# A recurrence's first stage moved beside the former pair's inverse: a re-ordered RWKV-7 hybrid step on one core

## The chip, the core and the metric

The kernel runs on one core of a Trainium2 chip. The metric is the device time of one launch in microseconds (us). Three runs of the kernel before gave 1659.1, 1659.86 and 1661.35 us; their median, 1659.86 us, is the time before. One further execution was profiled and took 1659.02 us.

## The reference, cut to what matters

One layer of a decoder trunk for 1024 prompt positions and 8 x 8 sample positions, 1088 columns in all, D = 1024, all in float32:

```python
h = rms_norm(x, norm_mix) * (1 + sc) + sh
P = h @ w_in                                   # RWKV columns, pooling columns, gates
xl = pr + (pr_prev - pr) * mu_shift
r, k, v, xw, xa, xg = split(xl)
decay = exp(-exp(-softplus(-(w0 + tanh(xw) @ w2)) - 0.5))
a = sigmoid(a0 + xa @ a2)
kk = heads(k * k_k);  kk = kk * rsqrt(sum(kk * kk) + 1e-12)
k = k * (1 + (a - 1) * k_a)
# per position t and head, state S (64 x 64):
S = S * w_t + (S @ -kk_t) (kk_t * a_t)^T + v_t k_t^T;   y_t = S r_t
# group norm of y, bonus, gate; merge with the pooling branch; w_out; then the MLP
```

What the change touches is the part from `k`, `xw` and `xa` to the products that the state update needs: the norm of `kk`, the two tanh of the low-rank maps (`w2` and `a2`), the running sums of the decay inside chunks of 64 positions, and the scaled copies of `k`, `kk * a`, `r` and `kk`.

## The kernel before, in words

Everything lies with features on the 128 partitions and positions along the free dimension. A large product is made from three matmuls on split operands (a rounded part `whi` and the rest `wlo`, lines 193 and 194), 362 or 364 columns at a time. These are called dense work here.

**Phase 1** streams w_in (34 blocks of 128 output columns, two weight halves each) and then the pooling half of w_br. **Phase 2** streams the other half of w_br, w_out and the MLP. The recurrence runs inside phase 1. It takes the 8 heads as four pairs, f = 0 to 3 (64 + 64 partitions), and the prompt as 16 chunks of 64 positions; the sample positions are a 17th chunk.

**The order of the work.** The order of TensorE's instructions is the program's own (`tc.manual_schedule(engines={PE})`), and a small planner writes it. `Pace.run` has one backlog of dense work and four generators: `chains`, `heads`, `pools` and `or_rows`. It keeps a clock `t`, to which each matmul adds an estimated cost. A generator that yields a number becomes due that many nanoseconds later on this clock; one that yields a condition becomes due when it holds. Whoever is due is resumed, the first in the list first; if nobody is due, the backlog emits three more matmuls. `warm(t)` is a condition that waits for `t` nanoseconds and for enough matmul work in the last 3400. The order on the other engines and on the DMA queues is made by the compiler's scheduler from the instructions as they were emitted.

**One pair.** `heads` (line 1143) goes through the pairs one after the other. For pair f:

- `lead` is `front(f)` and then `scores(f)`. Beside it runs `sample(f - 1)`, the sample positions of the pair before.
- `front` (line 648) loads `k`, `xw` with `xa`, and `r` from scratch memory; squares `k` (line 660), makes the norm by 18 narrow matmuls in `rinv` (line 345), spreads it by 9 transposes (line 177) and multiplies (line 672); makes the two low-rank maps in three column pieces with two tanh each (lines 677 and 680); waits for `("c", f - 1, 0)`, the end of the first half of the former pair's chain; and then emits, without a pause, the burst: for each half of the columns a sum (697), a scan (698), two or three Exp on ScalarE (700 to 703), and seven more VectorE instructions (706 to 711). After the first half `ra` (line 724) makes the first operands of `scores`. Its last step loads `v` and multiplies `q` (721).
- `scores` runs unit 0, the bonus, unit 2 (the sample chunk) and unit 1. Unit 0 starts its first matmul 9000 ns after `ra`.
- Then `main`, which is `inverse` (15 short VectorE steps), `level` (four rounds of 32 x 32 matmuls) and `affine` (`first` and `second` for each half), runs beside a fill: `post(f - 1)` for the former pair's group norm and gate, or `ada_fill` for f = 0. `both` is the helper that runs two generators side by side.
- `chain(f)` (line 964) steps the state through the 16 chunks, one step each 2300 ns of the planner's clock (line 994).

At the end come `sample(3)` and `post(3)`.

**Buffers.** The small products write PSUM tiles with the tag `w`, of which there are two; dense work has four (`mm`), and the chain has two (`wc`). `wt` is a ring of five 128 x 1088 tiles that `front`, `post` and the bonus share. `bk` and `e` have one buffer each; `ra` of the prompt has two.

## Time and profile before

| What | Value |
|---|---|
| median of 3 runs | 1659.86 us |
| the profiled execution | 1659.02 us |
| its span, first to last instruction | 1657.2 us |
| mean granted TensorE clock | 0.990 |
| TensorE busy (matmul) | 1599.2 us, 96% |
| VectorE busy | 1034.0 us, 62% |
| ScalarE busy | 712.7 us, 43% |

Each row of a view tells one thing. "PE" is TensorE's matmuls, "DVE" VectorE, "ACT" ScalarE, "POOL" GpSimd, "SP" the queue that issues most DMAs. In a timeline a row is: start in us, duration in us, engine, line, operation, output<-inputs, shapes, count, and in brackets the engine's idle time before it with what ended it. In a table by stretches the columns are: the stretch, its length, the busy time of each engine with its instruction count, the granted share of the TensorE clock, the share of the DMA engines and GB/s. In a table of waits: who waited <- for whom: us in total, times, longest.

### The profile page before, as it was taken

How to read it: one execution, taken by the hardware profiler on the slowest of the kernel's cores; microseconds unless marked ns; L12 is line 12 of the kernel's file. 1: busy time of each engine (PE TensorE's matmuls, PEld its weight loads, DVE VectorE, ACT ScalarE, POOL GpSimd, SP SyncE). 2: the span in 40 equal slices, each digit the busy share in tenths (PEclk: the TensorE clock that was granted, in tenths of full speed). 3: DMA queues.
4: the chain of work that ended last, by engine and by line, in shares of the span. 5: the costliest groups of instructions: out<-in, count | busy, mean ns of one | idle time of the engine just before them, and what ended most of it. 6: DMA issues, size and time to landing. Idle time of an engine off the chain costs nothing.

```text
span 1657.2 us, 35379 instructions
## 1 busy us (share of the span) xinstructions
PE 1599.2 (96%) x14331; PEld 1490.2 (90%) x14331; DVE 1034.0 (62%) x1800; ACT 712.7 (43%) x1378; POOL 354.5 (21%) x459
## 2 busy tenths in 40 slices
PE   6999999999999999999999999999999999999997
PEld 3989888887888889979989999999999999999997
DVE  5686547744675456335545596777555667776866
ACT  5543333344334334412224376455444656552323
POOL 3310111110000000000631333323233343521221
PEclk9999999999999999999999999999999999999999
DMA  9333413331322142375975455666766866574313
GB/s 337 112 110 133 139 53 117 114 105 64 115 107 101 70 149 88 117 294 177 330 280 195 144 186 172 234 227 232 238 218 212 311 202 217 174 257 167 98 39 109
DMA packets 123332, 279.42 MB, mean 169 GB/s; under 512 B 16769, under 2 KB 31105, under 8 KB 123169
## 3 DMA queue, kind: packets, MB, share of 16 engines
q1 hardware_dynamic: 107808, 228.52, 40.4%
q0 software_dynamic: 9312, 32.41, 6.0%
q10 hardware_dynamic: 6048, 16.23, 2.8%
q8 instruction: 113, 1.85, 0.5%
q14 instruction: 51, 0.41, 0.1%
HBM read 198.15 MB, written 78.95 MB: 167 GB/s over the span
## 4 chain that ended last, share of the span: by engine, by line
PE 59%; POOL 2%; DVE 2%; issue 2%; DMA 2%; ACT 1%; DVEq 0%; SPq 0%; POOLq 0%; ACTq 0%
PE pr L170 32%; PE mm L170 20%; PE w L170 5%; PE wc L170 2%; POOL t L1367 1%; POOL wlo L194 1%; DMA wraw<-in_w_ff 1%; DMA hid<-in_w_ada_mlp 0%; DMA hid<-d_th 0%; PE w L177 0%; DVE hx L1898 0%; DMA wr<-in_w_ff 0%; ACT whi L193 0%; POOL hx L1336 0%; DMA wraw<-in_w_br 0%
## 5 line engine op out<-in xcount | busy, mean ns | idle before, releaser
L170 PE MATMUL mm<-hx,whi 128*128 128x362 f32 (+1 forms) x1920 | 507.9, 346 | 6.2 <-ACT px L564 2.9
L170 PEld LDWEIGHTS mm<-hx,whi 128*128 128x128 f32 x1920 | 334.1, 190 | 42.6 <-issue 18.0
L170 PE MATMUL pr<-mr,whi 128*128 128x272 f32 x1792 | 337.5, 287 | 1.0 <-ACT whi L193 0.7
L170 PE MATMUL mm<-hx,wlo 128*128 128x362 f32 (+1 forms) x960 | 316.2, 329 | 0.0
L170 PEld LDWEIGHTS pr<-mr,whi 128*128 128x128 f32 x1792 | 281.7, 189 | 3.1 <-issue 2.2
L170 PE MATMUL pr<-mr,wlo 128*128 128x272 f32 x896 | 258.5, 289 | 2.8 <-DVE wlo L194 2.8
L193 ACT ACTIVATE whi<-wraw 128x512 fp32r<-128x512 f32 x186 | 116.7, 629 | 251.3 <-PE mm L170 73.4
L170 PEld LDWEIGHTS mm<-hx,wlo 128*128 128x128 f32 x960 | 182.9, 191 | 0.0
L194 DVE TENSOR_TENSOR wlo<-wraw,whi 128x512 fp32r<-128x512 f32 x145 | 108.8, 751 | 106.0 <-ACT whi L193 105.0
L170 PEld LDWEIGHTS pr<-mr,wlo 128*128 128x128 f32 x896 | 169.3, 189 | 3.0 <-DVE wlo L194 3.0
L170 PE MATMUL pr<-hx,whi 128*128 128x272 f32 x896 | 168.7, 287 | 1.4 <-DVE rs L1924 0.8
L170 PE MATMUL mm<-mr,whi 128*128 128x272 f32 (+4 forms) x736 | 152.7, 302 | 0.7 <-DVE t L1363 0.7
L170 PEld LDWEIGHTS pr<-hx,whi 128*128 128x128 f32 x896 | 140.3, 188 | 2.6 <-ACT whi L193 1.0
L193 ACT ACTIVATE whi<-wr 128x512 fp32r<-128x512 f32 x138 | 86.2, 628 | 128.7 <-PE pr L170 94.0
L170 PE MATMUL pr<-hx,wlo 128*128 128x272 f32 x448 | 128.9, 288 | 0.0
L170 PEld LDWEIGHTS mm<-mr,whi 128*128 128x128 f32 x736 | 119.2, 188 | 4.9 <-issue 3.4
L170 PE MATMUL mm<-mr,wlo 128*128 128x272 f32 (+4 forms) x368 | 110.1, 299 | 0.0
L194 POOL TENSOR_TENSOR wlo<-wraw,whi 128x512 fp32r<-128x512 f32 x41 | 55.6, 1356 | 250.7 <-ACT whi L193 250.4
L194 DVE TENSOR_TENSOR wlo<-wr,whi 128x512 fp32r<-128x512 f32 x103 | 77.4, 755 | 16.7 <-ACT whi L193 16.4
L170 PE MATMUL pr<-t,whi 128*128 128x272 f32 x448 | 84.6, 287 | 0.0
L170 PEld LDWEIGHTS pr<-hx,wlo 128*128 128x128 f32 x448 | 84.3, 188 | 0.0
L170 PEld LDWEIGHTS pr<-t,whi 128*128 128x128 f32 x448 | 70.2, 188 | 0.8 <-issue 0.8
(398 smaller groups left out, 2681.2 us busy)
## 6 DMA issues: line engine op xcount, KB each, us to landing
wr<-in_w_ff SPq DMA_DIRECT2D x137, 256.0 KB, 3.5
hid<-d_ch POOLq DMA_DIRECT2D x72, 272.0 KB, 4.2
wraw<-in_w_ff SPq DMA_DIRECT2D x71, 256.0 KB, 3.2
wraw<-in_w_in SPq DMA_DIRECT2D x68, 256.0 KB, 2.9
d_ch<-hx SPq DMA_DIRECT2D x52, 272.0 KB, 3.7
hid<-in_w_ada_mlp SPq DMA_DIRECT2D x24, 512.0 KB, 6.5
d_th<-px SPq DMA_DIRECT2D x22, 544.0 KB, 2.9
wt<-d_x SPq DMA_DIRECT2D x20, 544.0 KB, 4.1
```

The costliest lines, as they stand in the source:

```text
L170: return self.nc.tensor.matmul(out, lhsT, rhs, **kw)
L193: nc.scalar.activation(hi, raw, AF.Copy)
L194: (nc.gpsimd if pool else nc.vector).tensor_tensor(lo, raw, hi.bitcast(F32), op=ALU.subtract)
L1367: (nc.vector if m == 7 else nc.gpsimd).tensor_tensor(t, t, S["u"], op=ALU.add)
```

## The change

`front` is cut in two. What loads, norms and makes the tanh stays `front`; the burst becomes a generator of its own, `burst`, which for f > 0 yields between its steps. `heads` runs `front(0)` ahead of the loop and `front(f + 1)` behind `post(f - 1)` in the fill beside `main`; the lead is then `burst(f)` and `scores(f)`. The pause after each tanh piece is 2600, 1900 and 1900 ns for 1300 three times. For f > 0 the wait for the former pair's chain and the first `ra` stand at the end of the burst, and unit 0 starts 3000 ns after it for 9000. In `affine`, one of the three copies out of PSUM goes from VectorE to ScalarE.

```diff
             nc.scalar.activation(tha[:, c0:c0 + n], ps[:, :n], AF.Tanh, bias=self.hp[:, 4 + f:5 + f], scale=0.5)
-            yield 1300
+            yield 1900 if c0 else 2600
         yield X(f)
         r = self.wt()
         nc.sync.dma_start(r, self.d_x[f])
+        self.cur = dict(k=k, kk=kk, t1=t1, tha=tha, r=r)
+
+    def burst(self, f):
+
+        nc, io = self.nc, self.io
+        X = lambda b: lambda: ("X", b) in self.done
+        k, kk, t1, tha, r = (self.cur[x] for x in ("k", "kk", "t1", "tha", "r"))
+        step = lambda t: t if f else 0
         e = self.row(self.p1, "e", 1, w=1112)
...
-        if f:
-            yield lambda: ("c", f - 1, 0) in self.done
         for c0, n in FH:
...
             nc.vector.tensor_tensor_scan(t, self.kscan[:, s], t, 0.0, ALU.mult, ALU.add)
+            yield step(1800)
...
             for h, hs in enumerate(HB):
+                yield step(1700)
                 nc.vector.tensor_tensor(bk[hs, cs, h, :], cut(x[hs]), cut(t[hs]), op=ALU.mult)
...
             if c0 == 0:
                 self.cur = dict(bk=bk, end=end, kk=kk, r=r, ev=ev, es=es, z=self.z, qs={})
-                self.ra(self.cur, 0)
+                if f == 0:
+                    self.ra(self.cur, 0)
+            yield step(1400)
...
         self.cur.update(q=q, v=v)
+        if f:
+            yield lambda: ("c", f - 1, 0) in self.done
+            self.ra(self.cur, 0)
...
-        yield 9000 if u == 0 else 3000 if u == 1 else 2000
+        yield (3000 if f else 9000) if u == 0 else 3000 if u == 1 else 2000
...
-            nc.vector.tensor_copy(uv[HB[1], :, 0, :], cut(pu[HB[1], :]))
+            nc.scalar.activation(uv[HB[1], :, 0, :], cut(pu[HB[1], :]), AF.Copy)
...
+        yield from self.front(0)
         for f in range(4):
             def lead():
-                yield from self.front(f)
+                yield from self.burst(f)
                 yield from self.scores(f, self.cur)
...
-            fill = self.post(f - 1) if f else self.ada_fill()
             self.ds[f] = d
+
+            def fill():
+                yield from self.post(f - 1) if f else self.ada_fill()
+                if f < 3:
+                    yield from self.front(f + 1)
...
-            yield from self.both(main(), fill)
+            yield from self.both(main(), fill())
```

## The prediction, made before the changed kernel ran

> **What bounds the kernel now.** First the page, its part on busy time.

> ```profile
> PE 1599.2 (96%) x14331; PEld 1490.2 (90%) x14331; DVE 1034.0 (62%) x1800; ACT 712.7 (43%) x1378; POOL 354.5 (21%) x459
> ```

> TensorE (PE) works almost all the time, and the change takes no matmul away and adds none. So nothing can be won but time in which PE waits, or in which its clock is not granted in full; a shorter recurrence does not pay by itself. That second point must be checked at the end of phase 1, in the timelines of DVE and PE there.

> ```profile
> 775.73 0.76 DVE L1133 TENSOR_TENSOR hx<-wt,hx 128x576 fp32r<-128x576 f32 x1 [0.75 <-ACT hx L1132]
> ...
> 784.38 0.49 PE L170 MATMUL w<-hx,whi 128*128 128x362 f32 x2
> ```

> The recurrence's last result is written at 776.5 us; the first product that reads such rows (its third chunk goes to a `w` tile) is there at 784.38, some 8 us later. If the recurrence ends earlier nothing is won, and if it ends more than about 8 us later PE is left without work.

> Next the view by stretches: the three leads, from the end of `affine` of pair f - 1 to unit 0 of pair f, and a stretch that is nearly all dense.

> ```profile
> 219.00:264.00 45.00, 41.08 (x340) 32.84 (x338) 33.08 (x60) 17.74 (x38) 7.27 (x10) 0.96 0.20 64
> 385.00:429.20 44.20, 38.57 (x308) 29.90 (x306) 27.74 (x51) 16.25 (x33) 2.44 (x3) 0.92 0.30 97
> 545.50:592.50 47.00, 44.79 (x380) 36.24 (x379) 28.70 (x56) 16.53 (x35) 0.73 (x2) 0.93 0.20 65
> 740.00:780.00 40.00, 40.00 (x245) 39.02 (x244) 20.50 (x35) 10.27 (x18) 3.84 (x3) 1.00 0.53 182
> ```

> In the leads PE is idle for 3.9, 5.6 and 2.2 us, 11.7 in all, and the clock (the column behind POOL) sinks to 0.96, 0.92 and 0.93. The dense stretch has neither. What PE waited for over the whole span, and three of these waits in PE's timeline:

> ```profile
> PE w L170 <- ACT wt L677: 5.7, 8, 2.0
> PE wc L170 <- DVE S L994: 4.3, 4, 2.8
> PE mm L170 <- ACT px L564: 2.9, 3, 1.8
> ...
> PE w L170 <- DVE wt L1115: 1.9, 2, 1.0
> ...
> PE mm L170 <- ACT px L582: 1.6, 1, 1.6
> ...
> PE w L170 <- ACT at L944: 0.6, 1, 0.6
> ```

> ```profile
> 244.98 0.33 PE L170 MATMUL w<-x,z 64*64 64x64 f32 x4 [2.05 <-ACT wt L677]
> ...
> 425.15 0.48 PE L170 MATMUL wc<-S,ra 64*64 64x64 f32 x4 [2.80 <-DVE S L994]
> ...
> 581.24 0.34 PE L170 MATMUL w<-ab,uv 128*64 128x64 f32 x4 [0.58 <-ACT wt L677]
> ```

> The first three rows are the leads' causes. The two `w` tiles are held until the tanh of line 677 has read them: six of the eight waits, from 244.98 to 581.24, are those of the sample's products, the other two stand in the first front. The chain's step (line 994) stands behind the burst on DVE. And dense chunks are copied out late by ACT (564). Where the clock is lost, by stretches on PE:

> ```profile
> 220.00:240.00 20.00, 20.00 (x139) 0.91 0.19 62
> 234.00:237.40 3.40, 3.40 (x19) 0.50 0.14 50
> 401.20:404.60 3.40, 3.40 (x19) 0.50 0.64 204
> 425.10:428.50 3.40, 3.35 (x17) 0.50 0.75 199
> 561.65:568.48 6.83, 6.83 (x31) 0.50 0.04 14
> ```

> Four stretches at half clock in the leads: 17.0 us, so at most 8.5 us lost.

> **The change, part by part.** The sum is made against the profiled execution: 1659.02 us, of which 1657.2 are span and 1.8 lie around it. It stands 0.8 us under the median of the runs, 1659.86.

> *The front moves.* PE's timeline shows where it stands and where it can go.

> ```profile
> 359.53 0.27 PE L177 MATMUL w<-kct,sw 128*128 128x128 f32 x1
> ...
> 382.02 0.28 PE L170 MATMUL w<-ab,at 64*64 64x128 f32 x2
> ...
> 393.62 2.06 PE L170 MATMUL w<-kct,wt 128*128 128x2 f32 x18
> ...
> 412.79 0.76 PE L170 MATMUL w<-wt,sw 64*128 64x288 f32 x4
> ```

> `post` of pair 0 has its last transpose at 359.5 and its last writes some 3 us later; `affine` of pair 1 ends at 382, the next front's norm is at 393.6, its last tanh piece at 412.8, unit 0 at 429.2. After the change the front starts behind `post`, so its norm comes near 374 (11.6 us after its start, as now from 382 to 393.6). Its last piece is 19 us later, and 2.5 us more for the longer pauses: near 395, where the lead starts. The burst's pauses are 2 x (1.8 + 1.7 + 1.7 + 1.4) = 13.2 us, with each of the eight resumptions half a microsecond late some 17; then 3 us to unit 0: near 415, 14 us earlier than 429. Over three pairs the recurrence gets some 35 to 40 us shorter, which is worth nothing at the end of phase 1: the same dense work stands alone behind it. The loads hardly move, since the compiler has them ahead already, in the queue's timeline:

> ```profile
> 364.11 0.42 SPq L658 DMA_DIRECT2D wt<-d_x x1
> ```

> This load of `k` is issued 29 us before the norm at 393.62. I cost the DMAs at nothing: the five `wt` tiles are taken in the same order as before, and what SP holds behind a late load is the next weights, of which two are ahead; if that cover fails, it costs the dense work 1 or 2 us a pair.

> *Waits that go.* (a) The tanh's waits: beside the burst, which uses no `w`, the sample meets none, and the first front has the longer pauses: -5.7 us, between 0 and -5.7. (b) The chain's step waits because the whole burst was emitted ahead of it on DVE; in steps, it leaves room: -4.3, 0 to -4.3. (c) Dense chunks copied late are half a matter of what ACT happens to do: -1.4, 0 to -2.9. (d) The clock: the stretches at 234 and 561 follow the front's 18 narrow matmuls, those at 401 and 425 the stalls of 1.8 and 2.8 us. The narrow matmuls stay, the stalls should go; I take half, -4, between 0 and -8.5.

> [...]

> (e) The copy of line 945, by its own entry and that of the ScalarE copy behind it:

> ```profile
> L945 DVE COPY uv<-w x8: 694/695/695, 202.6 to 701.0; 64x512 f32<-64x512 f32 x8
> L946 ACT ACTIVATE uv<-w x8: 585/590/592, 203.4 to 701.8; 64x512 f32<-64x512 f32 x8
> ```

> 0.69 us on DVE become 0.59 on ACT, eight times. Behind it on ACT stand copies of dense chunks, for which PE waited 1.6 us once (line 582). ACT now does three copies in a row, but needs no longer wait for DVE between two of them: -0.5, from -1.6 to +2.

> *Waits that come.* (f) The front's ten `w` tiles a pair now meet `affine`, each stage of which takes both: the same kind of collision with another partner. Nothing before shows it; the nearest rows are the tanh's 5.7 us in all, and the waits of `post` and `affine` beside each other (1115, 944), 0.6 to 1.0 us each. I take two a pair at 1 us, +6, the row nearest to it; between 0 and +16 (five a pair). (g) The lead becomes short for DVE; I take +2, from 0 to +17, as weighed below. The wait for the former chain, moved behind the burst, has only `ra` and unit 0 queued behind it in its generator; where it comes late, it delays the recurrence, which has those 35 us to spare, and PE does dense work meanwhile: nothing.

> Sum: -5.7 - 4.3 - 1.4 - 4 - 0.5 + 6 + 2 = -7.9 us: 1651.1 for an execution like the profiled one, 1651.9 beside the median. **I predict 1651.5 us.**

> **The rivals.** *DVE becomes the bound of the lead* (slower). In the lead at 385 DVE is busy for 27.74 us; some 2 us of it, the norm's multiplies, move out with the front. The lead shrinks to 20 us. If the burst began only with it, DVE would be 27.7 - 2 - 20 = 5.7 us behind at unit 0, and PE would wait for that in each pair: 17 in place of (g)'s 2, so -7.9 + 15 = +7.1: 1666. What decides is where the burst starts on DVE. Against the rival: its first instruction (697) already runs ahead of its place in the program, in the timelines of DVE and PE,

> ```profile
> 244.87 0.43 DVE L697 TENSOR_SCALAR wt<-wt 128x512 f32<-128x512 f32 x1 [0.52 <-ACT wt L677]
> 251.53 0.76 PE L170 MATMUL w<-wt,sw 64*128 64x288 f32 x4
> ```

> right behind the first tanh and 6.7 us before the front's last piece. So it should start before the lead by about the 6 us that are missing.

> *The front collides with affine* (same, or slower): the upper end of (f), +16 for +6, gives 1661; if the narrow norm next to `affine`'s 64 x 64 products then costs the clock as often as now, 1665. For it: only two `w` tiles. Against it: the front's ten tiles are spread over 20 us.

> *Everything goes and nothing comes*: (a) to (e) at their far ends, -23, without (f) and (g): 1636; with one of the far ends missed, up to 1643.

> *The change does nothing that PE sees*: the loads were ahead already and waits only change partners: 1657 to 1662.

> **How the numbers follow.** The forecast's mechanism (1643 to 1656) has 0.55; everything goes 0.08; nothing that PE sees 0.15; DVE the bound 0.12; the front collides, and the clock with it, 0.10. 0.2% is 3.3 us, about what a measurement of this kernel can tell from no change: faster than 1656.5 has 0.63, within 0.15, slower than 1663.2 0.22. For 8 in 10 I leave out the larger half of the large gain and the far ends of the two slow cases: 1641 to 1665.

> **What would show it.** In the changed kernel the norm's 18 matmuls should stand before the end of `affine` or close to it, unit 0 some 12 to 15 us earlier in each pair, and the recurrence's last write 30 us or more before the product that reads it. The waits of PE for line 677 should be near 0 and those for 994 under 1 us; new waits for `w` tiles, if any, name lines 944 to 946, 960, 677 or 672. Fewer than 17 us at half clock inside phase 1 show (d). I am wrong if PE waits more than 2 us a pair at unit 0 or at line 994 with DVE busy throughout, or if the waits for `w` tiles beside `affine` pass 10 us.

## The result and the profile after

The changed kernel takes 1682.16 us (median of 4 runs, 1680.51 to 1682.45) against 1660.61 us for the kernel before in the same comparison (4 runs, 1659.1 to 1661.95). The ratio is 1.0129, with a 95% interval of 1.011 to 1.0149: 21.6 us slower, where 8 us faster was forecast. The profiled execution of the kernel after took 1682.03 us with a span of 1680.3, so 23.1 us more of span.

The page of the kernel after, busy time:

```profile
PE 1610.0 (96%) x14331; PEld 1498.0 (89%) x14331; DVE 1025.8 (61%) x1792; ACT 714.6 (43%) x1384; POOL 353.5 (21%) x459
```

The same 14331 matmuls keep TensorE busy for 10.8 us longer. The same matmuls with longer records point to a lower clock or to waits inside the records, so both are looked for below. Where the time went by, first at the end of phase 1, in the timelines of VectorE and TensorE after:

```profile
778.39 0.76 DVE L1146 TENSOR_TENSOR hx<-wt,hx 128x576 fp32r<-128x576 f32 x1 [0.79 <-ACT hx L1145]
...
805.06 0.49 PE L170 MATMUL w<-hx,whi 128*128 128x362 f32 x2
```

The first product of phase 2 went from 784.38 to 805.06 us: 20.7 of the 23.1 us are lost in phase 1. It doesn't wait for the recurrence, whose last write ended 26 us earlier. So the loss is time that TensorE spent badly while dense work and recurrence ran side by side. The remaining 2.4 us lie in phase 2, where one stretch of 6.83 us at half clock (963.60, shown below) can account for 3.4 at most.

The stages of phase 1 by stretches, before and then after. Columns: the stretch, its length, busy time with the count for PE, PEld, DVE, ACT and POOL, then the granted clock.

```profile
182.00:218.00 36.00, 36.00 (x770) 31.44 (x771) 9.33 (x16) 13.12 (x25) 2.19 (x7) 1.00 0.29 99
...
341.00:382.00 41.00, 37.56 (x784) 33.91 (x785) 18.31 (x32) 17.76 (x34) 2.54 (x3) 1.00 0.32 101
...
506.00:547.00 41.00, 38.73 (x776) 34.48 (x778) 19.41 (x34) 19.31 (x34) 0.00 (x0) 0.96 0.34 121
...
706.00:784.00 78.00, 76.78 (x566) 68.41 (x567) 34.86 (x67) 17.22 (x34) 5.11 (x4) 1.00 0.66 234
```

```profile
182.00:225.00 43.00, 39.51 (x781) 33.95 (x783) 12.15 (x22) 20.41 (x36) 2.30 (x7) 0.94 0.24 82
225.00:260.00 35.00, 31.73 (x283) 25.32 (x277) 27.61 (x50) 11.15 (x27) 5.79 (x8) 0.98 0.24 75
...
340.00:390.00 50.00, 42.84 (x782) 38.71 (x767) 14.57 (x24) 24.69 (x41) 0.10 (x1) 0.90 0.24 81
390.00:429.00 39.00, 32.01 (x254) 24.75 (x255) 29.38 (x57) 9.79 (x24) 2.85 (x6) 0.91 0.20 60
...
509.00:552.00 43.00, 40.47 (x771) 37.11 (x759) 18.60 (x33) 19.06 (x36) 1.65 (x2) 0.96 0.29 95
552.00:590.00 38.00, 36.47 (x299) 28.04 (x299) 27.98 (x53) 14.42 (x30) 0.71 (x2) 1.00 0.30 104
...
708.00:805.00 97.00, 95.17 (x683) 86.10 (x675) 35.64 (x71) 22.04 (x44) 5.30 (x5) 1.00 0.63 226
```

The stretches with 770 to 784 matmuls are `level` and `affine`, beside which the front now stands. They had 0, 3.4 and 2.3 us without a matmul before (the length less PE's busy time), and have 3.5, 7.2 and 2.5 now, at a clock of 0.94, 0.90 and 0.96 for 1.00, 1.00 and 0.96. They do the same number of matmuls in 7, 9 and 2 us more. The leads (254 to 299 matmuls) got shorter, 35, 39 and 38 us for the 45, 44 and 47 that the prediction showed, but not better: 3.3, 7.0 and 1.5 us without a matmul. What was taken out of them is dense work, which now stands at the end: 97 us with 683 matmuls for 78 with 566. So the change moved time from the leads to the stages before them and to the tail, and phase 1 got 21 us longer.

What PE waited for in phase 1, after (whom <- whom: us in total, times, longest), and two rows of the same view before that the prediction did not need:

```profile
PE wc L170 <- DVE S L1007: 7.0, 5, 2.6
PE w L170 <- ACT wt L677: 5.4, 4, 2.1
PE w L170 <- ACT iv L813: 5.0, 6, 1.7
PE w L170 <- issue: 3.8, 2, 3.4
PE w L170 <- ACT wt L660: 3.6, 1, 3.6
...
PE w L170 <- ACT at L957: 1.2, 2, 0.6
PE w L177 <- ACT at L957: 1.2, 2, 0.6
PE mm L170 <- ACT px L564: 1.0, 1, 1.0
```

```profile
PE w L170 <- DVE px L612: 1.3, 1, 1.3
...
PE w L170 <- ACT iv L800: 0.3, 1, 0.3
```

(Lines behind the change are shifted: 994 is 1007 now, 800 is 813, 944 is 957.) All rows of this view together, from 42 us to the end of phase 1, are 24.4 us before and 36.3 after. The tanh of line 677 still makes PE wait, the chain's step more than before, and two rows are new: the norm waits for the Square of line 660, and the sample's products wait for the score copies of line 813.

How this looks in one pair, from PE's timeline after:

```profile
366.78 4.00 PE L170 MATMUL w<-kct,wt 128*128 128x2 f32 x18 [3.56 <-ACT wt L660]
...
388.01 1.64 PE L170 MATMUL w<-ab,at 64*64 64x128 f32 x26 [2.11 <-ACT wt L677]
...
412.29 0.33 PE L170 MATMUL wc<-S,ra 64*64 64x64 f32 x4 [2.60 <-DVE S L1007]
...
417.28 1.55 PE L170 MATMUL w<-px,plw 128*128 128x364 f32 x2 [3.35 <-issue]
...
429.33 1.16 PE L170 MATMUL w<-ra,bk 64*128 64x128 f32 x16
...
432.47 0.34 PE L170 MATMUL w<-ab,uv 128*64 128x64 f32 x4 [0.91 <-ACT iv L813]
```

Five collisions in one pair (the row at 429.33 is unit 0). The first comes from the loads, in the timelines of the SP queue and of ScalarE after:

```profile
358.84 0.45 SPq L658 DMA_DIRECT2D wt<-d_x x1
```

```profile
366.00 1.39 ACT L660 ACTIVATE wt<-wt,part 128x512 f32<-128x512 f32 x2 [2.18 <-DMA wt<-d_x]
...
385.98 1.28 ACT L677 ACT_TABLE_LOAD   x1 [2.31 <-PE w L170]
```

The load of `k`, 29 us ahead of the norm before, is issued 8 us ahead of it now: the norm moved by 27 us and the load by 5. It stands between the last two stores of `post` in the same queue, as it did in the kernel before (that `post` holds the five `wt` tiles until then is the likely reason, and was not tried). Square starts 7.2 us after the issue. The second collision has `affine`'s products waiting for the `w` tile that the tanh holds, with a table load in front of it. In the third and fourth VectorE is full: the stretch shows it busy for 17.46 of 20 us, and two rows of its timeline the kind of work. The first is a long sum of the pooling between the chain's steps; the second ends 0.1 us before the pooling product at 417.28, for which the profile names no releaser.

```profile
400.00:420.00 20.00, 13.60 (x83) 9.87 (x82) 17.46 (x35) 3.94 (x10) 1.83 (x5) 0.85 0.25 75
```

```profile
404.22 1.23 DVE L601 TENSOR_TENSOR d<-px 128x1038 f32<-128x1038 f32 x1
...
417.03 0.15 DVE L612 COPY px<-zf 128x3 f32<-128x3 f32 x1
```

Then the clock, by the same view of stretches after:

```profile
362.86:366.27 3.41, 0.36 (x3) 0.05 (x1) 0.00 (x0) 1.22 (x3) 0.00 (x0) 1.00 0.96 372
366.27:376.51 10.24, 9.73 (x55) 9.33 (x57) 0.69 (x2) 4.41 (x8) 0.00 (x0) 0.50 0.05 19
...
963.60:970.43 6.83, 6.08 (x27) 5.79 (x27) 1.69 (x4) 1.29 (x2) 0.72 (x1) 0.50 0.27 86
```

A stretch of 3.41 us in which PE hardly works is followed by three at half clock. In phase 1 there are 34.1 us at half clock after and 20.5 before.

And unit 0, 14 us earlier by the forecast, stands where it stood in this pair (429.33 for 429.19); in the other two it is 3.8 and 3.0 us earlier. In the order of TensorE's program it did move. The stretch from 42 us to just before it, before and then after:

```profile
42.00:429.25 387.25, 371.07 (x3890) 326.53 (x3888) 243.18 (x440) 153.28 (x334) 51.96 (x105) 0.99 0.32 105
```

```profile
42.00:429.25 387.25, 361.95 (x3782) 317.55 (x3780) 236.55 (x431) 151.54 (x329) 48.96 (x104) 0.96 0.29 99
```

Some 108 fewer matmuls stand ahead of it, about 18 us of dense work at 0.17 us each (the median from start to start of the matmuls with 362 columns in phase 1 before). As much was lost by then: 9.1 us more without a matmul, and 27.3 us at half clock for 10.2, worth 8.5 at most. Its operands did not hold it, since the last of them is written 14 us earlier, in VectorE's timeline after:

```profile
414.55 0.68 DVE L746 TENSOR_TENSOR ra<-wt,e 128x512 f32<-128x512 f32 x1
```

The first product of the former pair's chain, in PE's timeline before and after, shows the same loss: behind practically the same number of matmuls (3512 and 3511 from 42 us on) it stands 12 us later.

```profile
377.67 0.33 PE L170 MATMUL wc<-S,ra 64*64 64x64 f32 x4
```

```profile
389.38 0.27 PE L170 MATMUL wc<-S,ra 64*64 64x64 f32 x2
```

So what the new order gained on unit 0 was given away again by waits and clock on the way there.

### The profile page after: what moved, and what is told of

Its sections match the earlier page's. It is cut to its first block, busy times and chain, and to the rows that moved or that the text cites. A ratio compares the mean times of both kernels' runs of the same rounds, so it can differ in the third digit from the quotient of the medians.

```text
span 1680.3 us, 35392 instructions
## 1 busy us (share of the span) xinstructions
PE 1610.0 (96%) x14331; PEld 1498.0 (89%) x14331; DVE 1025.8 (61%) x1792; ACT 714.6 (43%) x1384; POOL 353.5 (21%) x459
## 4 chain that ended last, share of the span: by engine, by line
PE 78%; DVE 7%; ACT 5%; DMA 4%; issue 3%; POOL 1%; SPq 0%; DVEq 0%; ACTq 0%; POOLq 0%
PE pr L170 32%; PE mm L170 31%; PE w L170 11%; PE wc L170 4%; DMA wraw<-in_w_out 2%; PE w L177 1%; ACT whi L193 1%; DVE wlo L194 1%; DMA x<-in_xT 1%; DMA wt<-d_x 1%; POOL t L1385 1%; POOL wlo L194 0%; DMA hid<-in_w_ada_mlp 0%; DVE d L601 0%; ACT iv L813 0%
## 5 line engine op out<-in xcount | busy, mean ns | idle before, releaser
L170 PE MATMUL mm<-hx,whi 128*128 128x362 f32 (+1 forms) x1920 | 508.6, 347 | 4.4 <-DVE px L1337 1.8
L170 PEld LDWEIGHTS mm<-hx,whi 128*128 128x128 f32 x1920 | 335.2, 191 | 40.2 <-issue 18.0
L170 PE MATMUL pr<-mr,whi 128*128 128x272 f32 x1792 | 337.7, 287 | 0.9 <-ACT whi L193 0.7
L170 PE MATMUL mm<-hx,wlo 128*128 128x362 f32 (+1 forms) x960 | 316.7, 330 | 0.2 <-DVE wlo L194 0.2
L170 PEld LDWEIGHTS pr<-mr,whi 128*128 128x128 f32 x1792 | 281.9, 189 | 3.0 <-issue 1.2
L170 PE MATMUL pr<-mr,wlo 128*128 128x272 f32 x896 | 258.8, 289 | 3.1 <-DVE wlo L194 3.1
L170 PEld LDWEIGHTS mm<-hx,wlo 128*128 128x128 f32 x960 | 183.5, 191 | 0.5 <-DVE wlo L194 0.5
L170 PEld LDWEIGHTS pr<-mr,wlo 128*128 128x128 f32 x896 | 169.3, 189 | 3.5 <-DVE wlo L194 3.5
L170 PE MATMUL pr<-hx,whi 128*128 128x272 f32 x896 | 170.2, 289 | 1.3 <-DVE rs L1942 0.8
L170 PE MATMUL mm<-mr,whi 128*128 128x272 f32 (+4 forms) x736 | 153.4, 303 | 0.0
L170 PEld LDWEIGHTS pr<-hx,whi 128*128 128x128 f32 x896 | 141.6, 190 | 2.7 <-ACT whi L193 1.0
L170 PE MATMUL pr<-hx,wlo 128*128 128x272 f32 x448 | 129.5, 289 | 0.0
L170 PEld LDWEIGHTS mm<-mr,whi 128*128 128x128 f32 x736 | 119.9, 190 | 3.8 <-issue 3.4
L170 PE MATMUL mm<-mr,wlo 128*128 128x272 f32 (+4 forms) x368 | 110.7, 301 | 0.0
L170 PEld LDWEIGHTS pr<-hx,wlo 128*128 128x128 f32 x448 | 85.0, 190 | 0.0
L170 PE MATMUL pr<-t,whi 128*128 128x272 f32 x448 | 84.6, 287 | 0.0
L170 PEld LDWEIGHTS pr<-t,whi 128*128 128x128 f32 x448 | 70.2, 188 | 0.8 <-issue 0.8
```

The lines of the kernel that those rows point to most:

```text
L170: return self.nc.tensor.matmul(out, lhsT, rhs, **kw)
```

## The experiments

Theories, as the expectations name them. **M**: the front's new place is dear in itself (a late load, `w` tiles shared with `affine`, half clock behind its narrow norm). **L**: the short lead is dear (VectorE full, the sample beside unit 0); for the kernels with the front still in the lead it was later put as a recurrence that gets longer and ends beyond the dense work. **O**: the loss is luck of the order; any new order of the instructions moves the time, and the parts don't add. Later came two suppositions on the clock: **D** (density), that it is halved after a stretch of 3.41 us with too few columns through PE, against **I**, that only idle gaps halve it. All times beside a fresh run of the kernel before; ratios have their 95% interval.

### The parts alone

**The front moved, nothing else**: burst in one piece behind the wait for the chain, pauses and copy as before. The main lines of the edit, against the kernel after:

```diff
-            yield 1900 if c0 else 2600
+            yield 1300
...
-        step = lambda t: t if f else 0
+        step = lambda t: 0
...
-        yield (3000 if f else 9000) if u == 0 else 3000 if u == 1 else 2000
+        yield 9000 if u == 0 else 3000 if u == 1 else 2000
```

> The front moved beside the former pair's post, level and affine, and nothing else of the change: the burst in one piece behind the wait for the chain, unit 0 after 9000, pauses of 1300, the copy on VectorE. Theory M (the front's new place loses the time: loads that land late, w tiles shared with affine, half clock): slower than before by 10 to 20 us, 1671 to 1681, with half-clock time in phase 1 over 27 us and a wait of PE for line 660. Theory L (the short lead loses it: VectorE full, the sample beside unit 0): within 6 us of before, 1655 to 1667, with no wait for 660. Theory O (any new order of TensorE's program moves the time by such an amount): anywhere from -10 to +15, and the parts do not add up.

Measured: 1681.95 us, ratio 1.0124 (1.0097 to 1.0151). This part alone is as slow as the whole change, 1 us above M's range and far above L's. Half clock in phase 1 is 41.0 us (over 27 expected by M); the wait for line 660 that M expected is not there. Its waits, in the same view:

```profile
PE w L170 <- issue: 8.9, 3, 7.3
PE wc L170 <- DVE S L1004: 6.2, 6, 2.5
```

The sum of its loss is that of the kernel after, the items are others: hardly a wait for the score copies (0.8 us), but 7.3 us in one piece in front of a pooling product. That already speaks against any single wait as the cause.

**Everything but the front's place**: `front(f)` stays in the lead, ahead of `burst(f)`.

```diff
-        yield from self.front(0)
...
             def lead():
+                yield from self.front(f)
                 yield from self.burst(f)
...
-                if f < 3:
-                    yield from self.front(f + 1)
```

> The whole change but the move: the front stays at the head of the lead, the burst goes in steps behind it, ra and unit 0 follow late, pauses 2600 and 1900, the copy on ScalarE. Theory M: at or under before, 1650 to 1661, since the tanh's and the chain's waits get smaller. Theory L: slower by 5 to 15 us, 1666 to 1676, with waits for lines 994 (the chain's step) and 800 (the copies of the scores) of over 8 us together. Theory O: anywhere from -10 to +15.

Measured: 1675.85 us, ratio 1.0088 (1.0063 to 1.0113). Slower too, against M. L's range holds the time, but its two waits sum to 6.2 us for the expected 8 or more. The loss comes by another way: the steps' pauses now lengthen the lead, the last `affine` ends at 751 us for 706, and the recurrence's end is no longer covered by dense work. The stretch at its end:

```profile
790.00:800.00 10.00, 7.07 (x27) 5.27 (x26) 3.95 (x8) 3.40 (x8) 0.00 (x0) 0.55 0.10 23
```

27 matmuls in 10 us at a clock of 0.55: that is `post(3)` with little beside it.

**The steps alone**: as the last, but with the old pauses between the tanh pieces and the copy on VectorE.

```diff
-            yield 1900 if c0 else 2600
+            yield 1300
...
-            nc.scalar.activation(uv[HB[1], :, 0, :], cut(pu[HB[1], :]), AF.Copy)
+            nc.vector.tensor_copy(uv[HB[1], :, 0, :], cut(pu[HB[1], :]))
```

> Of the change only the burst in steps with the short pause before unit 0; the front stays in the lead, the pauses are 1300 and the copy is on VectorE. With the longer pauses and the copy beside it (all_but_move) it was 1675.85. Theory L (the steps lengthen the recurrence so that its last pair ends beyond the dense work's end, and PE stands idle there): the end of affine of the last pair 35 us or more later than in the kernel before (706), some 10 us lost in the last 60 us of phase 1, 1668 to 1676. Rival: it was the longer pauses on top of the steps that did this; then steps alone end where before does, 1655 to 1662.

Measured: 1678.69 us, ratio 1.0108 (1.0076 to 1.014). So the steps and the short pause before unit 0 are dear by themselves while the front is in the lead. The last `affine` ends at 752 us, as L expects. By the working of the table below 4.7 us are lost behind 740 us, against 0.4 before; with every excess counted, also those under 0.4 us, it is some 12 of the 21 us. The time is 3 us above L's range; the rival, which put the loss on the longer pauses, falls.

**The longer pauses alone**, in the kernel before:

```diff
-            yield 1300
+            yield 1900 if c0 else 2600
```

> Before with the longer pauses behind the tanh pieces alone. All of theories M and L: within 6 us of before, 1655 to 1664; the waits of PE for line 677 fall from 5.7 us to under 4. Theory O: a shift of 5 to 10 us either way from this edit of four numbers alone.

Measured: 1653.52 us, ratio 0.9953 (0.9937 to 0.997). This is the one part that pays, and the kernel that beats both. But the time lies 1.5 us below the range of M and L and is a shift of O's size, and the waits for line 677, which were to fall under 4 us, went from 5.7 to 4.9 while those for the chain's step rose from 4.3 to 6.2. So where the 7 us come from is not shown.

**The copy alone**, in the kernel before:

```diff
-            nc.vector.tensor_copy(uv[HB[1], :, 0, :], cut(pu[HB[1], :]))
+            nc.scalar.activation(uv[HB[1], :, 0, :], cut(pu[HB[1], :]), AF.Copy)
```

> Before with the copy of line 945 on ScalarE alone; TensorE's order stays exactly the same. All theories: 1657 to 1662, no change over 2 us. If ScalarE is what holds the dense copies, up to 4 us slower.

Measured: 1657.38 us, ratio 0.9987 (0.9965 to 1.0008): no difference that can be told, in line with the -0.5 us of the forecast.

**Both**, pauses and copy, in the kernel before:

> Before with the longer pauses and the copy on ScalarE, the two parts that were measured at -7 and -3 us alone. If parts add: 1649 to 1653, faster than before by 7 to 11. Theory O: they do not add, anywhere from 1650 to 1662.

Measured: 1657.81 us, ratio 0.9986 (0.9967 to 1.0005). The gain of the pauses is mostly gone with the copy beside it. If parts of a fraction of a per cent added, 1649 to 1653 would have come out; here they didn't.

### The named waits taken away

**A later norm** in the kernel after, so that the loads are there:

```diff
-        yield self.pace.warm(8000 if f else 11000)
+        yield self.pace.warm(14000 if f else 11000)
```

> The changed kernel with one number more: the norm of the front beside the former pair's work starts after 14000 instead of 8000. So the norm stands behind affine's first stages, and its load of k has 6 us more to land. Theory M (late load, w tiles shared with affine, half clock): the wait for line 660 (3.6 us) and the 10 us at half clock behind it go, the excess beside level and affine falls from 47 us towards before's 33: 1668 to 1676. Theory L (sample beside unit 0, VectorE in the lead): no gain there, 1679 to 1685. Theory O (luck of order): a shift with no relation to these places.

Measured: 1680.11 us, ratio 1.0118 (1.0083 to 1.0154), from seven runs between 1670.61 and 1688.65. M's forecast (1668 to 1676) missed, L's (1679 to 1685) holds. The wait for line 660 is gone. In PE's timeline the same pair now reads:

```profile
378.35 3.02 PE L170 MATMUL w<-kct,wt 128*128 128x2 f32 x18 [1.27 <-DVE ra L974]
...
397.16 1.32 PE L170 MATMUL w<-wt,sw 64*128 64x288 f32 x2 [2.33 <-ACT wt L677]
```

The norm waits for `affine` instead, half clock follows at 379, and the tanh's wait stands behind `affine` rather than in it, with 13.7 us at half clock from 397. The 3.6 us came back as 2.3 us of clock (19.5 us lost at half clock for 17.2) and smaller waits.

**The sample before the scores**, in the kernel after: it runs beside the burst and is finished before unit 0.

```diff
             if f > 0:
-                yield from self.both(lead(), self.sample(f - 1, self.ds[f - 1]))
+                yield from self.both(self.burst(f), self.sample(f - 1, self.ds[f - 1]))
             else:
-                yield from lead()
+                yield from self.burst(f)
+            yield from self.scores(f, self.cur)
```

> The changed kernel, but the former pair's sample is finished beside the burst before the scores begin, so that none of its products meets unit 0. Theory L: the waits for line 813 (5.0 us) go and the excess in the units falls from 61 us towards before's 51: 1670 to 1678; the recurrence gets some 10 us a pair longer, of which its end has over 20 to spare. Theory M: within 4 us of the changed kernel. If the recurrence's end then lies behind the dense work, it is slower, over 1685, and the tail shows it.

Measured: 1682.11 us, ratio 1.0125 (1.0083 to 1.0167). The waits of the sample's products for the score copies fell from 5.0 us to 1.5, and the time did not follow: L's forecast missed, M's holds. In its views of waits and of PE's timeline:

```profile
PE w L170 <- ACT iv L813: 1.5, 2, 0.9
```

```profile
708.76 4.00 PE L170 MATMUL w<-kct,wt 128*128 128x2 f32 x18 [3.23 <-issue]
```

The recurrence became longer (last `affine` at 745 us for 708), and a group norm of `post` met `level` at 708, where 13.7 us at half clock began. One wait was removed, and what came behind it met others.

**Both repairs together:**

> The kernel after with both repairs of its named waits: the norm 14 us behind its loads, as in late_norm, and the sample finished before the scores start, as in sample_first. Alone they left the time at 1680.1 and 1682.1. If the waits named in the trace of after (660, and 813 at unit 0) were its loss, both together should give back their 9 us: 1672 to 1674. Theory O and theory D (the front beside affine thins out the columns per 3.41 us wherever its norm stands) expect the half clock to stay at 35 us or more and the time at 1677 to 1684.

Measured: 1668.93 us, ratio 1.0056 (1.0031 to 1.0081). Here, and only together, the two give back 13 us of the 22: more than the 9 of the named waits, and against the forecast of O and D, with 27.3 us at half clock for the 35 or more that these two expected. Still slower than before.

### The narrow norm broken up

The norm's matmuls three blocks at a time, each with its own small square root, so that dense chunks come between them:

```diff
-        ps = self.ps("w")
-        for i, b in enumerate(blocks):
-            self.mm(ps[:, 2 * i:2 * i + 2], x[:, b:b + 128], self.kc("hsel"), start=True, stop=True)
...
-        nc.scalar.activation(f, ps[:, :2 * k], AF.Sqrt, bias=self.eps[:, eps:eps + 1], scale=scale)
+        for a in range(0, k, 3):
+            m = min(3, k - a)
+            ps = self.ps("w")
+            for i in range(m):
+                b = blocks[a + i]
+                self.mm(ps[:, 2 * i:2 * i + 2], x[:, b:b + 128], self.kc("hsel"), start=True, stop=True)
+            nc.scalar.activation(f[:, 2 * a:2 * (a + m)], ps[:, :2 * m], AF.Sqrt, bias=self.eps[:, eps:eps + 1], scale=scale)
+            yield 900
```

In the kernel after:

> The kernel after, with the 18 narrow matmuls of each head pair's norm (and the 8 or 10 of the group norm in post) emitted three blocks at a time, 0.9 us of the planner's time apart, so that dense chunks come between them. Theory D (density): the clock of a stretch of 3.41 us is halved when PE streamed fewer than some 2800 columns in the stretch before; over the traces so far, 54 of the 55 such stretches in phase 1 were followed by half clock and 1 of several hundred above 3250. A norm of 36 columns over 3 to 4 us empties a stretch; broken up it does not. D expects the stretches at half clock in phase 1 to fall from 34.1 us to 24 or less and the time by 3 to 6 us: 1676 to 1679, ratio 1.009 to 1.012. Theory I (idle): only idle gaps of PE halve the clock; nothing at the norms changes, 1680 to 1684. Theory O (luck of order): half clock goes at the norms and comes back elsewhere, time within 3 us of the kernel after.

Measured: 1668.13 us, ratio 1.0042 (1.0022 to 1.0063): 14 us faster than the kernel after. In PE's timeline the pair that had 10.2 us at half clock behind one norm now has

```profile
387.75 0.83 PE L170 MATMUL w<-kct,wt 128*128 128x2 f32 x6
...
391.63 0.83 PE L170 MATMUL w<-kct,wt 128*128 128x2 f32 x6
```

and a third piece after these, and no half clock between 279 and 528 us. The direction is D's, the sizes are not: phase 1 has 27.3 us at half clock for 34.1 (24 or less was expected), 5.1 us less lost by it, and 8 us less in stalls, which D did not foresee. Theory I expected no change, and the count of columns in the last section speaks against it too.

In the kernel before, alone, and in the kernel before with the longer pauses:

> The kernel before with the norms three blocks at a time and nothing else. Theory D alone: the 20.5 us at half clock in phase 1 fall to 12, 1654 to 1658. The rival, after pauses_split: each break-up lengthens the lead on the recurrence's chain (two pauses of 0.9 us in the front's norm, six in post), the recurrence ends 40 us or more later (before: the last affine ends at 706) and meets the pooling products at the units, 1675 to 1690.

> The kernel before with the longer pauses between the tanh pieces (which alone gave a ratio of 0.9953) and with the norms emitted three blocks at a time, as in after_split. Theory D expects the 23.9 us at half clock in phase 1 to fall to some 14, and the time by 3 to 5 us more: 1648 to 1650, ratio 0.993 to 0.994. Theory I: 1652 to 1655. Theory O: anywhere from 1650 to 1660, since any new order moves the time by some 4 us.

Measured: 1665.31 us, ratio 1.0034 (1.0016 to 1.0053), and 1688.39 us, ratio 1.0169 (1.0137 to 1.02). Both of D's forecasts missed, the second by 38 us, and half clock rose in both, from 20.5 and 23.9 us to 30.7 and 37.5. In the old arrangement the pauses of the norm lie on the lead, the last `affine` ends at 728 and 755 us for 706, and the later units meet the pooling's products. Breaking up a stage helped only in the arrangement where it did not lengthen the lead.

In the kernel after together with the two repairs above:

> The kernel after with its three repairs: the norm 14 us behind its loads, the sample finished before the scores start, and the norms three blocks at a time. late_sample (the first two) was 1668.9, after_split (the third) 1668.1, after 1682.2. Theory M+D (the loss is these collisions and the half clock that thin stretches bring): what is left shrinks again, 1652 to 1662, at or below before, with under 20 us at half clock in phase 1. Theory O (luck of order): the parts don't add, 1665 to 1685.

Measured: 1681.49 us, ratio 1.0136 (1.0119 to 1.0153). Each of the two was worth 13 or 14 us alone, together they are worth nothing: the last `affine` is at 765 us and phase 1 has 51.2 us at half clock. This is O's number.

### How much is luck of the order

The pooling's first pause 300 ns longer on the planner's clock and nothing else, in the kernel before, in the kernel after, and in the kernel before with the longer pauses:

```diff
-            yield 6500 + 1300 * g
+            yield 6800 + 1300 * g
```

> Before with a pause of the pooling branch raised from 6500 to 6800: no part of the change, nothing that any theory of it prices; it only moves the order of TensorE's program from the first pooling product on. Theories M and L: within 3 us of before. Theory O: a shift of 4 us or more either way, which would be the size below which no edit of this order can be read.

> The kernel after with the pooling's first pause 6800 in place of 6500, as jitter_pool did to the kernel before, which stayed at 1659.9. Theory M: the front's place is the cause, the time stays at 1677 to 1685. Theory O: any new order moves the time of this arrangement, and 1682 was an unlucky one: 1665 to 1676.

> The kernel before with the longer pauses (1653.5 alone) and the pooling's first pause 6800 in place of 6500. If the gain of the longer pauses is of their own making (fewer waits for line 677 and for the copies), the time stays at 1650 to 1656; if it was luck of the order, it returns to 1657 to 1663.

Measured: 1659.85 us, ratio 1.0 (0.9981 to 1.0018); 1688.11 us, ratio 1.018 (1.0162 to 1.0197); 1656.24 us, ratio 0.998 (0.9967 to 0.9993). The old arrangement doesn't move, the new one moves by 6 us, to a value that neither theory had named. The gain of the longer pauses shrinks from 7 to 4 us, just beyond the upper edge of what was expected if the gain is of their own making; the interval is still below 1.

### All of them in one table

Worked out from the traces of all 18 kernels: for every matmul of phase 1, the time from its start to the next one's, less the median of that time for matmuls of its shape and tile over all traces. What exceeds it by over 0.4 us at full clock is a stall; the excess inside the stretches at half clock, up to 0.6 us a matmul, is lost by the clock. Columns: time, first product of phase 2, us at half clock in phase 1, us lost by it, stalls, end of the last `affine`.

```
before          1660.6  784.4  20.5  10.2  31.6  706
jitter_pool     1659.8  785.5  27.3  12.6  32.0  707
copy_alone      1657.4  781.6  20.5   9.6  29.7  703
pauses_alone    1653.5  781.2  23.9  11.6  27.0  706
pauses_copy     1657.8  781.6  17.1   7.3  31.7  706
pauses_jitter   1656.2  778.8  20.5  11.0  27.6  704
before_split    1665.3  793.0  30.7  11.2  36.4  728
pauses_split    1688.4  811.1  37.5  14.0  53.1  755
steps_alone     1678.7  805.9  37.5  13.2  48.9  752
all_but_move    1675.8  801.9  41.0  14.6  42.8  751
move_alone      1682.0  805.8  41.0  19.1  45.1  693
after           1682.2  805.1  34.1  17.2  45.0  708
after_jitter    1688.1  816.5  54.6  26.0  49.9  718
late_norm       1680.1  804.4  47.8  19.5  39.9  718
sample_first    1682.1  805.0  44.4  20.6  36.9  745
late_sample     1668.9  792.8  27.3  11.8  32.6  736
after_split     1668.1  793.3  27.3  12.1  36.9  720
all_repairs     1681.5  810.7  51.2  19.7  44.7  765
```

All eight kernels with the front beside the former pair's stages (the last eight rows) are slower than before, by 7 to 28 us. So the place costs something in every order that was tried: M in its direction. How much it costs is decided by the order, over a range of 20 us: O in the size. The losses of all_but_move and steps_alone come with a recurrence 45 us longer; the kernel after has none of that (708 for 706), so they are no part of its loss. One rival is left: before_split, pauses_split, steps_alone and all_but_move, where the front has not moved, are slower as well, by 5 to 28 us. That most large re-orders of this kernel lose, whatever they move, no run here excludes.

## Why the prediction was wrong

**What held.** PE is the bound, the end of the recurrence is not, and only waits and clock can be won or lost: 7.0 us more lost by the clock and 11.9 us more of waits make 18.9 of the 20.7 us of phase 1. The last write stands 26 us ahead of the product that reads it (30 or more forecast), but that is no merit of the mechanism: the write came 2.7 us later than before (779.2 for 776.5) and the product 20.7. The recurrence did not get 35 to 40 us shorter. The copy moved to ScalarE is worth nothing that can be told. VectorE did become full in the lead, as one rival had it, but its price, 1666, is not the story either.

**The step that failed is "the front moves"**, with what was built on it: that the waits (a), (b) and (d) go because the front leaves the lead. Together they were to bring -14; they brought +9.4. Point by point, from the waits of phase 1 before and after:

- *The place in time.* The norm came even earlier than forecast (366.78 for 374), and the last tanh piece stands at 394.90 (395 forecast). From there to unit 0 it took 34.4 us for the forecast 20, and unit 0 did not move. The estimate took the pauses of the planner's clock for real time; that clock counts neither a wait nor a lower TensorE clock, and of both there was more in the new order than in the old. "The wait for the former chain ... nothing" was right: in the program's order the chain's half is done 5 to 13 us of the planner's clock before the burst reaches that wait, in all three pairs.
- *(a) The tanh's waits*, -5.7 forecast: 5.4 us remain, -0.3. The premise that the tanh meets nobody who uses `w` was true of the sample and left out `affine`, which waits 2.1 us for the tile in the pair shown.
- *(b) The chain's step*, -4.3 forecast: +2.7. In steps the burst leaves room on VectorE, but the change puts the sample's reductions and the pooling's long sums (1.2 us each) into the same 20 us.
- *(c) The dense copies*, -1.4 forecast: lines 564 and 582 gave 3.5 us, two other rows took back 1.7 (line 531 +1.1, line 1337 +0.6).
- *(d) The clock*, -4 forecast: +7.0. The norm's narrow matmuls left a lead in which dense work stood beside them, and went to `affine`, whose matmuls of 64 and 128 columns are thin as well. The prediction put two of its four stretches at half clock behind the narrow matmuls, with PE busy for 3.40 of 3.40 us in the one at 234, and then counted only what the stalls would give back, and nothing for what the norm's new neighbours would cost.
- *(f) Tiles against affine*, +6 forecast: +5.9 (line 660 +3.6, line 957 +1.8, line 974 +0.5), so the number is luck: the largest of these is no tile but the load, which was costed at nothing because it stood 29 us ahead before.
- *(g) VectorE in the short lead*, +2 forecast: +7.2 net (score copies +4.7, pooling products +3.8 of issue, less 1.3 of line 612). That the sample's products would wait for unit 0's score copies on ScalarE was not thought of.

The rest of the waits is -1.8. With (a) to (g) that is the +11.9.

**What the runs showed in its place.** Moving the front alone costs as much as everything together (1.0124). It does not work through one wait: taking away the load's wait or the sample's wait leaves the time where it was, both together bring 13 us, the norm in pieces 14, all three nothing. What is common to its eight orders is that two chains of short products stand side by side where before a chain ran beside dense work; that a late item of either then stops PE, or thins it out enough to halve the clock, is the reading that fits the rows of the pair shown, not one that a run isolates. The forecast's rival "the front collides with affine" had the direction, but 1661, or 1665 with the clock, for 1682: it counted the collision in tiles alone.

**What stays open.** Why one order of the new arrangement gives 1668 and another 1688 was not taken apart further than into stalls and clock, and the rival of the last section, that most large re-orders lose here, stands. That a still better order of it lies below 1660 is not excluded; none of eight showed it.

## What to carry to other kernels

When a kernel is bound by an engine that is busy 96% of the time, ask of a moved stage what it meets where it arrives, not only what it clears where it leaves; here the front, a chain of short matmuls, left dense work and met another chain. A price list of waits is no sum when one removed wait shifts all that follows; for gains under 1% test the parts alone, and test the winner once more with a harmless shift of the order. Here the small part (longer pauses between pieces that share two buffers) paid, 0.9953 and still 0.998 after the shift, and the rearrangement around it did not.

## What the runs showed of the hardware

```profile
230.56:233.97 3.41, 3.41 (x33) 3.21 (x32) 2.46 (x6) 1.90 (x4) 0.00 (x0) 1.00 0.12 23
```

```profile
230.69 0.33 PE L170 MATMUL wc<-S,ra 64*64 64x64 f32 x4
230.86 0.28 PE L170 MATMUL wc<-ra,S 64*64 64x64 f32 x4
231.07 2.17 PE L170 MATMUL w<-kct,wt 128*128 128x2 f32 x18
233.10 0.58 PE L170 MATMUL mm<-hx,whi 128*128 128x362 f32 x2
233.52 0.33 PE L170 MATMUL mm<-hx,wlo 128*128 128x362 f32 x1
233.68 0.55 PE L170 MATMUL mm<-hx,whi 128*128 128x362 f32 x2
```

PE is busy for 3.41 of 3.41 us (by the profile's modelled ends of matmuls), yet the moving operands have 8 x 64 + 18 x 2 + 5 x 362 = 2358 columns; dense work, at 0.17 us for 362, streams some 7250 in that time. The 18 narrow matmuls take 2.17 us for 36 columns. Counted so over the 18 traces, from 42 us to the end of phase 1, each matmul in the stretch of the grid in which it starts: full-clock stretches by their columns, and how many were followed by half clock.

```
columns        stretches   followed by half clock
under 2500         80          78
2500 to 2750       26          24
2750 to 3250       43          15
3250 to 4000      116           6
over 4000        3526           1
```

Of these 124, 33 stand behind a stretch in which PE was without a matmul for less than 0.3 us. Columns are the measure that sorts the stretches here; what the chip itself counts, no run shows. Half clock came with the 3.56 us of waiting ahead of 366.78, and it also came behind the 2358 columns without a gap.

**A planner's time and real time drift apart where waits are.** The pauses of 13.2 and 3 us, of the burst and behind it, took 34.4 us from the last tanh piece (394.90) to unit 0 (429.33), with the waits and the half clock shown above.
